# Two small tiles are padded, and all large tiles begin at other addresses

## The chip, the cores and the metric

The kernel runs on one core of a Trainium2 chip. The metric is device time in microseconds of one execution, taken as the median of several runs; lower is better. TensorE (PE) multiplies, VectorE (DVE) and ScalarE (ACT) work elementwise, and SyncE (SP) issues the transfers from memory (HBM) to the on-chip memory. A tile has 128 partitions (rows) and a number of bytes in each; "address" below means the byte offset of a tile within each partition, and "residue" that offset modulo 512.

## What is computed

A trunk of two decoder layers over 512 tokens of width 1024, all in float32. Layer 0 mixes tokens with a Mamba-2 block (SSD), layer 1 with HGRN2; each layer has a squared-ReLU MLP and a gate by an embedding of its own:

```python
for i in range(DEPTH):                       # DEPTH = 2
    mix = ssd_mixer(x, ...) if i % 2 == 0 else hgrn2_mixer(x, ...)
    h = layer_norm(DEEPNORM_ALPHA * x + mix, ln_g[i, 0], ln_b[i, 0])
    h = layer_norm(DEEPNORM_ALPHA * h + sq_relu_mlp(h, mlp_w1[i], mlp_w2[i]), ln_g[i, 1], ln_b[i, 1])
    x = h + jax.nn.sigmoid(h @ ple_w_gate[i]) * (p[i] @ ple_w_proj[i])

def sq_relu_mlp(h, w1, w2):
    a = jax.nn.relu(h @ w1)                  # 1024 -> 4096
    return (a * a) @ w2
```

SSD projects to 5152 columns, convolves, computes decayed scores in chunks of 128 tokens for 32 heads, norms and projects back. HGRN2 projects to 4096 columns and works on 8 heads with a decay for each key channel, then norms and gates.

## The kernel before

Almost all time goes into products of weights and activations. For precision each operand is split into a high and a low part of type float32r, and a product is made of three matmuls that accumulate in one bank of PSUM (helper `mm3`, lines 110 to 112: high by high, high by low, low by high). In a matmul one operand is stationary (loaded into the array, 128 columns at a time) and the other moves through it, 512 or 256 columns at a time.

- `unit` (line 98) brings a weight unit of 128 x 1024 values: a transfer into a slot `raw`, a copy by ScalarE into `whi` (line 104), the rest by VectorE into `wlo` (line 106). There are 3 slots of raw and 5 each of whi and wlo.
- Activations lie transposed and split in slots of `b8` (9 slots of 8192 bytes, class `Split`).
- `project` takes the weights as stationary and b8 as moving operand; `out_part` takes b8 as stationary and whi or wlo as moving operand.
- In the MLP of each layer most pairs of hidden tiles are made with Strassen's scheme (`strassen`, 7 products of 256 columns for 8). Four of its seven left factors are sums of blocks: three of them lie in the tiles `S`, the fourth in a slot of b8; the other three are read from b8 as they are.
- The HGRN phase has its order on TensorE written out by hand: the projections of later heads fill the waits of a head's scores (`fill`, `need`, `background`). Its 128-column products (line 782: scores; lines 869, 880, 882: states and outputs) are plain float32, and the profile shows two records for each. In the SSD phase lines 522, 561, 591 and 596 are of the same kind; transposes (lines 200, 516, 549 and others) go through TensorE with `ident` from the constants as moving operand.

Tiles come from pools. The pools `consts`, `raws`, `whip`, `wlop`, `b8`, `accp`, `w4` and `sm` are placed one behind another in the order in which they are opened, and last the pool of the temporaries of the running phase (`tmp`: xs, sz, cv, cm, cbm, z, S, y, pv and so on), which is exchanged at each phase. Each tile's place is rounded up to 32 bytes. Two of the small tiles are `one`, a column of ones in `consts` (used as a bias when `ones_r` is filled), and `hri`, four reciprocals per head of HGRN in `sm`, which has two slots for each of its names.

Of the kernel before, what the change touches and what calls it, by code (L numbers as in the profile page):

```python
# [15 lines left out]
P = 128  # L16
T = 512
NCH = 4
# [11 lines left out]
# the first pairs of hidden tiles are plain products, the others Strassen's  # L30
PLAIN = 3
ORDER = [(w[0], int(w[1])) for w in "h0 b0 h1 o0 h2 o1 h3 o2 h4 o3 h5 o4 h6 o5 h7 o6 o7".split()]
# HGRN: the projections in their order, and how much of them goes between the steps of two heads
# [9 lines left out]
def trunk(ctx: ExitStack, tc, a):  # L43
# [9 lines left out]
    sm = pool("sm", 2)  # L53
# [21 lines left out]
    def begin(name):  # L75
        """the pool of temporaries of a phase, in place of the phase before's"""
        if phase:
            phase[1].__exit__(None, None, None)
            phase.clear()
        phase.append(tc.tile_pool(name=name, bufs=1, reuse_waits="tile"))  # L80
        phase.append(phase[0].__enter__())
        phase.reverse()
        phase.append(bufs[name])
# [13 lines left out]
    # ---------------------------------------------------------------- weights  # L97
# [16 lines left out]
    class Split:  # L114
        """[128, n, 512] as high and low parts, in slots of four rows each."""
# [11 lines left out]
    def project(src, xs, ps, m=P, tok=slice(0, T)):  # L127
        """ps[m, tok] = W[:, tile].T @ x.T for a weight unit of eight row tiles."""
        hi, lo = src
        for k in range(8):  # L130
            c = slice(k * m, (k + 1) * m)
            mm3(ps[:m, tok], hi[:, c], lo[:, c], xs.h(k, tok), xs.l(k, tok), k == 0, k == 7)

    # ---------------------------------------------------------------- constants
# [30 lines left out]
    one = mk(cpool, [P, 1], "one")  # L165
# [4 lines left out]
    # ---------------------------------------------------------------- layer norm and friends  # L170
# [7 lines left out]
    def layer_norm(c, gb):  # L178
        """acc[:, c] = LN(acc[:, c])"""
        src = acc[:, c, :]  # L180
        st = mk(sm, [P, 2, 6], "lnst")
        for h in range(2):
            nc.vector.bn_stats(st[:, h, :], src[:, h * 512 : (h + 1) * 512])
        mv = mk(sm, [P, 2], "lnmv")
        nc.vector.bn_aggr(mv, st.rearrange("p a b -> p (a b)"))
        sd = mk(sm, [P, 1], "lnsd")
        nc.scalar.activation(sd, mv[:, 1:2], AF.Sqrt, bias=eps)
        rs = mk(sm, [P, 1], "lnrs")
        nc.vector.reciprocal(rs, sd)
        nc.vector.scalar_tensor_tensor(src, src, mv[:, 0:1], gb[0], ALU.subtract, ALU.mult)  # L190
        nc.vector.scalar_tensor_tensor(src, src, rs, gb[1], ALU.mult, ALU.add)

    def transpose_split(src, dst, c, keep=None):
        """dst[:, k, chunk c] = src[tokens, k-th 128 features].T, split; unsplit in keep"""
        sl = slice(c * P, (c + 1) * P)
        for q in range(2):
            pt = bank(pst, "pt")
            for j in range(4):
                k = 4 * q + j
                nc.tensor.transpose(pt[:, j * P : (j + 1) * P], src[:, k * P : (k + 1) * P], ident)  # L200
            v = pt.rearrange("p (j t) -> p j t", j=4)
            h = dst.hi[q][:, :, sl]
            nc.scalar.copy(h, v)
            nc.vector.tensor_sub(dst.lo[q][:, :, sl], v, f32(h))
            if keep is not None:
                nc.scalar.copy(keep[q][:, :, sl], v)

    def out_part(units, n, xs, c, h, first, scale):
        """acc[:, c, half h] += x[:, chunk c].T @ W over n row tiles, each token's row by scale if given;
        acc holds alpha * residual (or the residual, if first)"""  # L210
        sl = slice(c * P, (c + 1) * P)
        ps = bank(psj, "pj")
        for k in range(n):
            hi, lo = units[k // 2]
            ks = slice((k % 2) * 512, (k % 2 + 1) * 512)
            mm3(ps, xs.h(k, sl), xs.l(k, sl), hi[:, ks], lo[:, ks], k == 0, k == n - 1)
        d = acc[:, c, h * 512 : (h + 1) * 512]
        if scale is not None:
            nc.vector.scalar_tensor_tensor(d, ps, scale[:, c : c + 1], d, ALU.mult, ALU.add)
        elif first:  # L220
            nc.vector.scalar_tensor_tensor(d, d, ALPHA, ps, ALU.mult, ALU.add)
        else:
            nc.vector.tensor_add(d, ps, d)  # L223

    def out_project(w, xs, first, after=None, scale=None):
        """w: the four units of four row tiles, by halves of the columns; after(c): what follows the last of chunk c"""
        if after is not None:
            units = [unit(w[i]) for i in range(4)]
            for c in range(NCH):
                for h in range(2):  # L230
                    out_part(units[2 * h : 2 * h + 2], 4, xs, c, h, first, scale)
                after(c)
        else:
            for h in range(2):
                units = [unit(w[2 * h + i]) for i in range(2)]
                for c in range(NCH):
                    out_part(units, 4, xs, c, h, first, scale)

    def norm(i):
        """the norm's result, transposed and split, and what makes its chunk c"""  # L240
        gb = ln_params(i)
        h_s = Split(8)
        keep = [mk(b8, [P, 4, T], "b8") for _ in range(2)] if i % 2 == 0 else None

        def chunk(c):
            layer_norm(c, gb)
            transpose_split(acc[:, c, :], h_s, c, keep)

        return h_s, chunk, keep

    # Winograd's form of Strassen's product: seven products of blocks for eight. The blocks of h.T are
    # [token half][k half], those of the weights [k half][output tile].
    def block_sums(h_s, ht):
        """the four plain and four summed blocks of h.T, as (high, low) of a row tile k"""
# [28 lines left out]
    def weight_sums(src1, src2):  # L283
        """the seven blocks of two weight units: B11, B21, B22, T1, T2, T3, B21 - T2, as (high, low, column)"""
# [24 lines left out]
    def strassen(blocks, src1, src2, z):  # L309
        """z[:, m] = W[:, tile m].T @ h.T for two weight units"""  # L310
# [34 lines left out]
    def mlp_and_gate(layer, h_s, ht, last):  # L345
        """acc holds the normed h. Returns the next x, transposed and split, with x in acc."""
# [40 lines left out]
        # gate  # L387
# [45 lines left out]
    # ---------------------------------------------------------------- layer 0: SSD  # L433
    # time steps
# [36 lines left out]
    # dt * exp(cs_last - cs)  # L471
# [6 lines left out]
    def dt_tail():  # L478
        # token-major copies: [128 tokens, chunk, head]
# [10 lines left out]
    def conv_silu(ps, i, out):  # L490
        """out = silu(causal conv of ps + bias), channel tile i of the convolved ones"""
        cv = tmp("cv", [P, T])
        nc.scalar.activation(cv, ps, AF.Identity, scale=convw[:, i, 3:4], bias=convb[:, i : i + 1])
        for k in range(3):
            d = 3 - k
            nc.vector.scalar_tensor_tensor(cv[:, d:], ps[:, : T - d], convw[:, i, k : k + 1], cv[:, d:], ALU.mult, ALU.add)
        nc.scalar.activation(out, cv, AF.Silu)
# [44 lines left out]
    def core(j, xs, sz, y, toks, btok, cbm, cm):  # L542
# [3 lines left out]
        # token-major x * dt and x * dt * decay to the chunk's end  # L546
# [11 lines left out]
        # chunk states and their scan  # L558
# [13 lines left out]
        # masked decays times C B  # L572
# [9 lines left out]
        # decay from the chunk's start, on channels  # L582
# [33 lines left out]
    def rms_group(ss):  # L616
        """1 / rms of each token of the group: [128 tokens, chunk]"""
# [52 lines left out]
    # ---------------------------------------------------------------- layer 1: HGRN2  # L670
# [6 lines left out]
    # lower bounds: softmax over the one layer, cumulated, less its first row  # L677
# [11 lines left out]
    # The tensor engine's order is fixed here: the projections of the heads to come fill the waits of a head's scores.  # L689
    def vg(i):  # L690
        """values and output gates of heads 2i and 2i + 1, by tokens: [128, chunk, 256]"""
# [80 lines left out]
    def hcore(h, s, i, hl):  # L772
# [12 lines left out]
        def column_sums(f, n):  # L785
            """the sums over the partitions, on each of them"""
# [8 lines left out]
        # the scores of a token with itself and of an odd one with the token before it  # L795
# [63 lines left out]
        # states  # L859
# [23 lines left out]
        # norm and output gate  # L883
# [5 lines left out]
        ri = mk(sm, [P, NCH], "hri")  # L889
# [51 lines left out]
def _tiles_m(w):  # L941
    """[K, M] -> [M/128, 128, K/128 * 128]: one unit per 128 output channels"""
# [4 lines left out]
def _tiles_g(w):  # L947
    """[K, 1024] -> [K/128, 128, 1024]: per four row tiles, two units for each half of the columns"""
# [5 lines left out]
def _tiles_h(w):  # L954
    """[K, 1024] -> [2 * K/256, 128, 2 * 512]: by halves of the columns, two row tiles each"""
# [5 lines left out]
def _tiles_q(w):  # L961
    """[1024, 1024] -> [4, 2, 128, 4 * 256]: by quarters of the columns, four row tiles each"""
# [4 lines left out]
def _cols(v):  # L967
    """[n * 128] -> [128, n]"""
# [3 lines left out]
def _rows(v):  # L972
    """[K, T] -> [128, K/128, T]"""
# [70 lines left out]
```

## Time and profile before

| | us |
|---|---|
| median of 3 runs | 1495.58 |
| lowest and highest run | 1493.39, 1496.82 |
| the profiled execution: span from its first to its last instruction | 1492.3 |
| TensorE busy in it | 1479.3 (99%) |
| VectorE busy | 1096.4 (73%) |
| ScalarE busy | 711.2 (48%) |

The page gives no other time for the profiled execution than its span; the runs lie 1.1 to 4.5 us above it. The granted TensorE clock is full (0.999 on average). Groups of the profile are read as: line, engine, operation, tile written <- tiles read (the moving operand of a matmul first), shape, count | busy time in us, mean ns of one | idle time before them. A matmul's own duration is a latency, and matmuls overlap; how fast they follow each other is read from their starts in the timeline. The name `b` in a row stands for a slot of b8 or for the second tile of w4.

The SSD phase takes roughly the first 350 us, the MLP and gate of layer 0 go up to about 790, HGRN up to about 1090, and the MLP and gate of layer 1 fill the rest.

### The profile page before, as it was taken

To read this page: it belongs to the slowest core of one execution; us is meant where nothing else is said; L and a number is where in the kernel's file an instruction comes from. 1 tells how busy PE (TensorE), PEld (TensorE's weight loads), DVE (VectorE), ACT (ScalarE), POOL (GpSimd) and SP (SyncE) were. 2 spreads that over 40 slices of the span, in tenths; PEclk is the share of its full clock that TensorE was granted. 3 is DMA by queue.
4 is the path that set the end of the run, shared out by engine and by line. 5 is a ranking of instruction groups with operands and counts; after the bars stand their busy time and mean duration, and the time that the engine had idled before them with its cause. 6 is when DMAs were issued, how large, how long until landed. Compare 5 with 4: busy or idle time off the path is not lost.

```text
span 1492.3 us, 21964 instructions
## 1 busy us (share of the span) xinstructions
PE 1479.3 (99%) x8848; PEld 1280.9 (86%) x8848; DVE 1096.4 (73%) x1786; ACT 711.2 (48%) x968; POOL 0.9 (0%) x8
## 2 busy tenths in 40 slices
PE   8999999999999999999999999999999999999998
PEld 5888888888989999888778998989898999998887
DVE  6998677797886777776844767769787777777673
ACT  5777455563564434444334453543364444444342
POOL 0000000000000000000000000000000000000000
PEclk9999999999999999999999999999999999999999
DMA  6433223332233323244223222222123333324322
GB/s 237 169 102 111 98 100 113 100 113 85 71 99 99 113 82 103 88 139 129 94 71 114 86 66 77 70 72 72 57 72 99 114 113 100 110 79 150 115 71 71
DMA packets 41621, 150.07 MB, mean 101 GB/s; under 512 B 4624, under 2 KB 5136, under 8 KB 41392
## 3 DMA queue, kind: packets, MB, share of 16 engines
q1 hardware_dynamic: 41520, 148.67, 30.1%
q8 instruction: 70, 1.15, 0.3%
q14 instruction: 31, 0.25, 0.1%
HBM read 146.49 MB, written 2.16 MB: 100 GB/s over the span
## 4 chain that ended last, share of the span: by engine, by line
PE 97%; DMA 1%; DVE 1%; ACT 1%; issue 0%; SPq 0%; ACTq 0%; DVEq 0%
PE pj L110 29%; PE pj L111 28%; PE pj L112 28%; PE py L782 1%; PE py L591 1%; PE pt L200 1%; PE pm L561 1%; PE py L596 1%; PE py L792 1%; PE py L827 1%; DMA raw<-in_wg 1%; DVE wlo L106 0%; PE pt L549 0%; PE py L880 0%; PE py L112 0%; PE py L110 0%
## 5 line engine op out<-in xcount | busy, mean ns | idle before, releaser
L110 PE MATMUL pj<-whi,b 128*128 128x512 f32 (+1 forms) x1096 | 401.5, 367 | 0.5 <-ACT z L414 0.5
L111 PE MATMUL pj<-wlo,b 128*128 128x512 f32 (+1 forms) x1096 | 399.3, 364 | 0.5 <-DVE wlo L106 0.5
L112 PE MATMUL pj<-whi,b 128*128 128x512 f32 (+1 forms) x1096 | 399.8, 365 | 0.0
L110 PE MATMUL pj<-b,whi 128*128 128x256 f32 (+1 forms) x1024 | 348.0, 340 | 2.1 <-ACT whi L104 2.1
L112 PE MATMUL pj<-b,wlo 128*128 128x256 f32 (+1 forms) x1024 | 344.2, 336 | 0.0
L111 PE MATMUL pj<-b,whi 128*128 128x256 f32 (+1 forms) x1024 | 343.7, 336 | 0.0
L104 ACT CAST whi<-raw 128x1024 fp32r<-128x1024 f32 x192 | 201.4, 1050 | 229.6 <-PE pj L111 133.4
L106 DVE TENSOR_TENSOR wlo<-raw,whi 128x1024 fp32r<-128x1024 f32 x192 | 233.9, 1220 | 64.4 <-ACT whi L104 62.4
L111 PEld LDWEIGHTS pj<-wlo,b 128*128 128x128 f32 x1096 | 206.8, 189 | 32.2 <-DVE wlo L106 1.0
L110 PEld LDWEIGHTS pj<-whi,b 128*128 128x128 f32 x1096 | 206.6, 189 | 32.3 <-ACT z L414 0.7
L112 PEld LDWEIGHTS pj<-whi,b 128*128 128x128 f32 x1096 | 206.7, 189 | 31.7 <-issue 0.2
L110 PEld LDWEIGHTS pj<-b,whi 128*128 128x128 f32 x1024 | 194.5, 190 | 22.0 <-ACT whi L104 4.7
L112 PEld LDWEIGHTS pj<-b,wlo 128*128 128x128 f32 x1024 | 194.4, 190 | 20.3 <-DVE b L150 1.7
L111 PEld LDWEIGHTS pj<-b,whi 128*128 128x128 f32 x1024 | 194.6, 190 | 18.3 <-issue 1.9
L293 ACT CAST whi<-raw 128x1024 fp32r<-128x1024 f32 (+1 forms) x52 | 43.4, 835 | 136.2 <-PE pj L112 110.4
L223 DVE TENSOR_TENSOR acc<-pj,acc 128x512 f32<-128x512 f32 x120 | 81.6, 686 | 35.0 <-PE pj L112 34.5
L110 PE MATMUL pj<-S,whi 128*128 128x256 f32 x312 | 87.4, 280 | 0.0
L111 PE MATMUL pj<-S,whi 128*128 128x256 f32 x312 | 87.0, 279 | 0.0
L112 PE MATMUL pj<-S,wlo 128*128 128x256 f32 x312 | 87.0, 279 | 0.0
L295 DVE TENSOR_TENSOR wlo<-raw,whi 128x1024 fp32r<-128x1024 f32 (+1 forms) x52 | 49.7, 957 | 35.0 <-ACT whi L293 35.0
L293 ACT CAST whi<-a 128x1024 fp32r<-128x1024 f32 x26 | 27.3, 1050 | 94.8 <-PE pj L111 45.5
L110 PEld LDWEIGHTS pj<-S,whi 128*128 128x128 f32 x312 | 58.7, 188 | 0.0
(217 smaller groups left out, 1810.6 us busy)
## 6 DMA issues: line engine op xcount, KB each, us to landing
raw<-in_w SPq DMA_DIRECT2D x128, 512.0 KB, 3.4
raw<-in_wssd SPq DMA_DIRECT2D x40, 512.0 KB, 3.4
a<-csd SPq DMA_DIRECT2D x16, 512.0 KB, 4.0
raw<-in_wso SPq DMA_DIRECT2D x16, 512.0 KB, 3.3
raw<-in_wg SPq DMA_DIRECT2D x16, 512.0 KB, 3.8
raw<-in_whvg SPq DMA_DIRECT2D x16, 512.0 KB, 3.3
raw<-in_whq SPq DMA_DIRECT2D x16, 512.0 KB, 3.3
raw<-in_who SPq DMA_DIRECT2D x8, 512.0 KB, 3.3
```

Source lines behind the costliest of these rows:

```text
L104: nc.scalar.copy(hi[:, :n], raw[:, :n])
L106: nc.vector.tensor_sub(lo[:, :n], raw[:, :n], f32(hi[:, :n]))
L110: nc.tensor.matmul(out, sh, mh, start=start, stop=False)
L111: nc.tensor.matmul(out, sh, ml, start=False, stop=False)
L112: nc.tensor.matmul(out, sl, mh, start=False, stop=stop)
L200: nc.tensor.transpose(pt[:, j * P : (j + 1) * P], src[:, k * P : (k + 1) * P], ident)
L223: nc.vector.tensor_add(d, ps, d)
L293: nc.scalar.copy(hi[:, :n], f)
L295: nc.vector.tensor_sub(lo[:, :n], f, f32(hi[:, :n]))
L561: nc.tensor.matmul(pst_[:, c * P : (c + 1) * P], btok[:, c, :], xw[:, c].rearrange("p h q -> p (h q)"), start=True, stop=True)
L591: nc.tensor.matmul(yd[64 * r : 64 * r + 64, sl], xdt[:, 2 * c + r, :], m[:, r, sl], start=True, stop=True)
L596: nc.tensor.matmul(yo[:, c * P : (c + 1) * P], pv[:, c - 1].rearrange("p h q -> p (h q)"), cm[:, c * P : (c + 1) * P], start=True, stop=True,)
```

## The change

Two tiles are allocated larger than what is used of them; the used part is a view of the first columns. All other lines differ only in comments, which are left out.

```diff
-    one = mk(cpool, [P, 1], "one")
+    one = mk(cpool, [P, 16], "one")[:, 0:1]
     nc.gpsimd.memset(one, 1.0)
...
         nc.scalar.activation(ms, ms, AF.Sqrt, scale=1.0 / P, bias=eps)
-        ri = mk(sm, [P, NCH], "hri")
+        ri = mk(sm, [P, 64], "hri")[:, :NCH]
         nc.vector.reciprocal(ri, ms)
```

Four bytes of `one` become 64 in each partition, and 16 bytes of `hri` become 256, in each of its two slots. With the rounding to 32 bytes, the tiles behind `one` move by 32 bytes, and those behind `hri` by 448 more. The slots from `raws` to `w4` go from residue 480 to 0, those of the phase pools from 32 to 0.

## The prediction

> **What bounds the kernel now.** I read the page first (busy shares, then the chain that ended last), then the groups kept apart by shape, then single rows of the timeline, and last the windows.
>
> ```profile
> span 1492.3 us, 21964 instructions
> PE 1479.3 (99%) x8848; PEld 1280.9 (86%) x8848; DVE 1096.4 (73%) x1786; ACT 711.2 (48%) x968; POOL 0.9 (0%) x8
> PE 97%; DMA 1%; DVE 1%; ACT 1%; issue 0%; SPq 0%; ACTq 0%; DVEq 0%
> ```
>
> TensorE is busy for 99% of the span, and the chain of waits runs through it for 97%. So the time is the number of matmuls times the step from the start of one to the start of the next, plus some 45 us (3% of 1492.3) in which TensorE waits. A change that adds no work and removes none can only act through that step, or through those 45 us. The counts by shape:
>
> ```profile
> L110 PE MATMUL pj<-whi,b 128*128 128x512 f32 x824 | 323.4, 393 | 0.0
> L110 PE MATMUL pj<-b,whi 128*128 128x512 f32 x480 | 194.2, 405 | 2.1 <-ACT whi L104 2.1
> L110 PE MATMUL py<-whi,a 128*128 128x512 f32 x32 | 12.7, 398 | 0.0
> L110 PE MATMUL pj<-b,whi 128*128 128x256 f32 x544 | 153.7, 283 | 0.0
> L110 PE MATMUL pj<-whi,b 128*128 128x256 f32 x272 | 78.1, 287 | 0.5 <-ACT z L414 0.5
> L110 PE MATMUL pj<-S,whi 128*128 128x256 f32 x312 | 87.4, 280 | 0.0
> L591 PE MATMUL py<-b,xdt 128*64 128x128 f32 x256 | 22.0, 284 | 0.0
> L880 PE MATMUL py<-a,cm 128*128 128x128 f32 x64 | 11.0, 274 | 0.0
> L869 PE MATMUL pm<-a,btok 128*128 128x128 f32 x48 | 6.8, 278 | 0.5 <-DVE pv L873 0.5
> ```
>
> Helper mm3 issues each product three times (L110, L111, L112), so these rows stand for 3 x (824 + 480 + 32) = 4008 products of 512 columns, 3 x (544 + 272) = 2448 of 256 columns whose moving operand (the first name after the arrow) lies in a slot of b8, whi or wlo, and 3 x 312 = 936 of 256 columns whose moving operand is S. The mean ns of a row are latencies of overlapping matmuls; the step has to be read from the starts in the timeline:
>
> ```profile
> 802.95 0.39 PE L112 MATMUL pj<-b,wlo 128*128 128x512 f32 x1
> ...
> 809.75 0.39 PE L112 MATMUL pj<-b,wlo 128*128 128x512 f32 x1
> ```
>
> ```profile
> 408.95 0.28 PE L110 MATMUL pj<-b,whi 128*128 128x256 f32 x1
> ...
> 412.79 0.28 PE L112 MATMUL pj<-b,wlo 128*128 128x256 f32 x1
> ```
>
> ```profile
> 425.25 0.28 PE L110 MATMUL pj<-S,whi 128*128 128x256 f32 x1
> ...
> 429.38 0.28 PE L112 MATMUL pj<-S,wlo 128*128 128x256 f32 x1
> ```
>
> Between the two rows lie 30, 32 and 35 steps: 6.80/30 = 226.7 ns for 512 columns, 3.84/32 = 120.0 ns for 256 columns out of b8, 4.13/35 = 118.0 ns for 256 columns out of S. The first two give the price of a column, (226.7 - 120.0)/256 = 0.417 ns, hence 213.3 and 106.7 ns of pure streaming. What is left is the same for both widths: 13.3 ns a matmul, as long as 32 columns (128 bytes of a row). With S it is 118.0 - 106.7 = 11.3 ns. Over the kernel this fixed part is 4008 x 13.3 + 2448 x 13.3 + 936 x 11.3 = 53.3 + 32.6 + 10.6 = 96 us, the only large amount that a mere shift of addresses could touch.
>
> **The change, part by part.** The program places its tiles in the order of declaration, each rounded up to 32 bytes. From their sizes, the constants begin 128 bytes past a multiple of 512 (16,512 bytes in), and all slots from raws to w4 (raw, whi, wlo, b8, acc, a, b) at 480 past one; their sizes are multiples of 4096, so all share that residue. The tiles of the phases (S, xs, z and so on) begin at 32 past a multiple. Tile one grows from 32 to 64 bytes: everything behind it moves by 32, and the big slots land at residue 0. The two slots of hri grow from 32 to 256 bytes each: the phase tiles move by 32 + 448 = 480, and land at 0 too. No instruction is added, removed or moved: the memset of one still writes one column, and ri is still four columns wide. No wait is added, and nothing goes past SP's or POOL's queue. These edits cost nothing by themselves.
>
> What may change is what each access costs. The important fact is that the trace has products that differ in the residue of the moving operand: b8 at 480 costs 120.0 ns, S at 32 costs 118.0, with the same shape, the same weights tiles, the same three lines. So the start matters by nanoseconds. I take the simplest reading: the fixed part is mostly one surplus fetch because a row does not begin where a fetch begins, and it goes when it does. No product in the trace has a moving operand of the large kind on residue 0, so the saving has to be bounded:
>
> Upper bound, 512 columns: all 13.3 ns, to 213.3. For 256 columns another limit comes first. Each matmul has its own weight load, and the 128-column products, which stream for only 53 ns, show at what step loads follow each other:
>
> ```profile
> 849.54 1.05 PE L782 MATMUL py<-xs,cv 128*128 128x128 f32 x8
> 49.09 0.49 PE L516 MATMUL pt<-cst,bm 128*128 128x128 f32 x3
> ```
>
> Eight records in 1.05 us with some 0.275 for the last (0.274 and 0.278 in the rows above) make (1.05 - 0.275)/7 = 111 ns; the transposes of L516 make (0.49 - 0.275)/2 = 108 ns. I let the 256-column products stop at 111: 9.0 ns saved out of b8, 7.0 out of S. The upper sum is 4008 x 13.3 + 2448 x 9.0 + 936 x 7.0 = 53.3 + 22.0 + 6.6 = 82 us. Lower bound of the same reading: only what 480 against 32 shows, 2 ns on 6456 products = 13 us. From below nothing: if the start is not the reason, 0, and a loss is priced under the rivals. I take the upper sum as the pace, because a constant of exactly 32 columns that is the same at both widths looks like a unit of fetching and not like a remainder.
>
> The Trainium skill (TensorE: Matmul & The Clock Gate, "Wait — 56ns, not 53.3ns?") puts a back-to-back matmul at its columns over 2.4 GHz plus about 2.5 ns, measured in bf16. The trace agrees on the columns (0.417 ns each) and not on the rest (13.3 ns); if 2.5 ns stay, the 512-column term is 4008 x 10.8 = 43 us by that page instead of 53.3, and the sum 72 instead of 82.
>
> Not all of this arrives at the end, since TensorE then asks for weights and evictions sooner:
>
> ```profile
> 30.00:400.00 370.00, 369.97 (x2029) 303.03 (x2028) 301.96 (x564) 216.50 (x285) 0.00 (x0) 1.00 0.32 107
> 400.00:700.00 300.00, 300.00 (x1891) 272.70 (x1891) 220.66 (x306) 140.58 (x156) 0.00 (x0) 1.00 0.33 106
> 800.00:1090.00 290.00, 289.28 (x1972) 255.72 (x1971) 207.72 (x418) 130.69 (x260) 0.00 (x0) 1.00 0.22 72
> 1090.00:1400.00 310.00, 310.00 (x1977) 282.67 (x1976) 229.59 (x319) 144.73 (x162) 0.00 (x0) 1.00 0.33 108
> ```
>
> In these windows (columns: length, then busy PE, PEld, DVE, ACT, POOL, then clock, DMA share, GB/s) VectorE is busy for 302 of 370, 221 of 300, 208 of 290 and 230 of 310 us. A stage shorter by 6% leaves it at 87% in the first and at 78% at most in the others, so it does not become the bound; the clock is 1.00 throughout, and the DMA share about a third. But in the first and third window products wait in chains through VectorE and ScalarE, which do not get shorter, and the places where only a transfer counts (here the three longest) stay as they are:
>
> ```profile
> 729.14 4.47 DMA raw<-in_wg
> 760.41 3.58 DMA raw<-in_wg
> 790.45 3.83 DMA raw<-in_whq
> ```
>
> These rows are from the chain in order of time. The first and third window hold 370 + 290 = 660 of 1492 us, so some 44% of the 82 us, 36, are saved there; I let two fifths of that, 15 us, be given back to the chains (my choice; the ends are nothing and all of the 36). Net 67 us. Against the profile's span that is 1492.3 - 67 = 1425; the median of the runs, 1495.6, lies 3.3 us above the span, so **1428 us**.
>
> **The rivals.** First, the forecast in part (chance 0.23): the fixed part belongs to changing the weights, and only the 2 ns that tell S from b8, up to 5 ns, hang on the start. 2 to 5 ns on 6456 products are 13 to 32 us: 1464 to 1483 us, middle 1475. For it: S improves by only 2 ns although its start differs by 64 bytes. Against it: 13.3 is so exactly 32 columns.
>
> Second, no effect (0.14): the 13.3 ns are a switch between products, and S is quicker for another reason, such as its two parts lying in one tile; 1495.6. For it: in all these rows the residue of b8, whi and wlo is one and the same, so none shows a change of it. Against it: the transposes of L516, whose moving operand is a constant that begins 128 past a multiple of 512, step at 108 ns, the products of L782, whose moving operand begins 32 past one, at 111. The Trainium skill (SBUF — State Buffer, "Specifications (TRN2)") speaks for this rival: its lines are 16 bytes, and 480 and 32 are multiples of 16, so by that rule nothing begins askew now. The 2 ns between S and b8 are what the page does not explain. That the tiles do not land where I worked it out (0.03) gives the same time.
>
> Third, slower (0.16): what counts is not the start but the distance between the starts of the two streams, weights and moving operand, because both are fetched at once. Now S and whi lie 64 bytes apart and cost 118.0, b8 and whi at equal residues cost 120.0. After the change all residues are equal: the 936 S products pay 2 ns more, 1.9 us, and so may the 256 + 64 + 48 = 368 records of L591, L880 and L869, which mix an a or b slot (480) with a phase tile (32) and now get equal residues, at up to 4 ns (111 against 108): 1.5 us. That is 1495.6 + 3.4 = 1499. It decides where the extra exceeds 2.3 ns on these 1304 matmuls. Against it: the distances among the big slots stay what they are, so 6456 of the products keep theirs.
>
> **How the numbers follow.** A measurement of this kernel can tell about 0.2%, 3 us, from no change. Forecast 0.44, in part 0.23: faster 0.67. No effect 0.14 and not placed so 0.03: same 0.17. Slower 0.16. The forecast's own range reaches from 1404 to 1445: at the low end nothing is given back and the loads follow each other at 108 ns, which adds 3 x 3384 = 10 us (1495.6 - 92); at the high end 3 ns of the fixed part stay at 512 columns (12 us less) and 20 us are given back (1495.6 - 50). The range that should hold 8 in 10 goes from 1404 through the partial case to the top of no effect, 1497; it leaves out the slower case and a little below.
>
> **What would show it.** In the profile after: steps of 512-column products at 213 to 217 ns and of 256-column ones at 108 to 113, S equal to b8; PE still at 98 to 99% of a shorter span; the same counts of instructions; DVE's busy time about 1096 us and its share up by three points; the waits of raw<-in_wg no shorter. A step of 224 and 118 would be the partial case, 226.7 and 120.0 with S at 118.0 no effect, and S at 120.0 with the rest unchanged the slower rival. If PE's share falls under 96%, the give-back is mis-sized. The prediction is wrong as a whole if the step of the 512-column products does not move.

## The result and the profile after

The changed kernel takes 1497.32 us (median of 15 runs, 1494.92 to 1498.94) against 1494.67 us of the kernel before on the same chip (15 runs, 1492.72 to 1496.82): 1.0015 times the time, 95% interval 1.0008 to 1.0022. It is slower by 2.65 us, where 67 us less had been forecast. The profiled execution of it begins like this (span, busy shares, chain that ended last by engine):

```profile
span 1494.8 us, 21964 instructions
PE 1481.7 (99%) x8848; PEld 1283.0 (86%) x8848; DVE 1096.8 (73%) x1786; ACT 710.9 (48%) x968; POOL 0.9 (0%) x8
PE 97%; DMA 1%; DVE 1%; ACT 1%; issue 0%; SPq 0%; ACTq 0%; DVEq 0%
```

The counts are those of before, and the instructions of each engine stand in the same order. The span grew by 2.5 us (from 1492.3), TensorE's busy time by 2.4 us (from 1479.3): the loss is TensorE's. Apart by shape, in the view of the groups:

```profile
L110 PE MATMUL pj<-whi,b 128*128 128x512 f32 x824 | 323.3, 393 | 0.2 <-ACT whi L104 0.2
L110 PE MATMUL pj<-b,whi 128*128 128x512 f32 x480 | 194.4, 405 | 1.7 <-ACT whi L104 1.7
L110 PE MATMUL pj<-b,whi 128*128 128x256 f32 x544 | 153.7, 283 | 0.0
L110 PE MATMUL pj<-S,whi 128*128 128x256 f32 x312 | 88.3, 283 | 0.0
L591 PE MATMUL py<-b,xdt 128*64 128x128 f32 x256 | 22.0, 284 | 0.0
```

Of these only the row of S moves: 88.3 us instead of 87.4, and on mm3's two other lines 88.3 instead of 87.0. The other rows shown stand within 0.2 us. The timeline gives the step, first for 512 columns, then for 256 columns out of b8, then out of S:

```profile
803.69 0.39 PE L112 MATMUL pj<-b,wlo 128*128 128x512 f32 x1
...
809.81 0.39 PE L112 MATMUL pj<-b,wlo 128*128 128x512 f32 x1
```

```profile
408.73 0.28 PE L110 MATMUL pj<-b,whi 128*128 128x256 f32 x1
...
412.57 0.28 PE L112 MATMUL pj<-b,wlo 128*128 128x256 f32 x1
```

```profile
425.02 0.28 PE L110 MATMUL pj<-S,whi 128*128 128x256 f32 x1
...
429.11 0.28 PE L111 MATMUL pj<-S,whi 128*128 128x256 f32 x1
```

Between the rows lie 27, 32 and 34 steps: 6.12/27 = 226.7 ns, 3.84/32 = 120.0 ns, and 4.09/34 = 120.3 ns, where before stood 118.0. Over the whole trace 932 of the 936 S products step at exactly 120 ns. So what came is the third rival's picture: S became as slow as b8, and no other step changed by more than 0.2 ns in the mean. 936 x 2.1 ns = 2.0 us of the 2.5 us. The three longest waits for a transfer grew too, in the chain in order of time:

```profile
729.83 4.82 DMA raw<-in_wg
761.43 3.76 DMA raw<-in_wg
791.65 4.05 DMA raw<-in_whq
```

They were 4.47, 3.58 and 3.83 us, together 0.75 less. But they are not the rest: TensorE's idle time, span less busy time, grew only from 13.0 to 13.1 us. Where the other half microsecond lies, and whether it hangs on the change, no run shows.

### The profile page after: what moved, and what is told of

Read it like the earlier page. It is cut to its first block, busy times and chain, and to the rows that moved or that the text cites. A ratio compares the mean times of both kernels' runs of the same rounds, so it can differ in the third digit from the quotient of the medians.

```text
span 1494.8 us, 21964 instructions
## 1 busy us (share of the span) xinstructions
PE 1481.7 (99%) x8848; PEld 1283.0 (86%) x8848; DVE 1096.8 (73%) x1786; ACT 710.9 (48%) x968; POOL 0.9 (0%) x8
## 4 chain that ended last, share of the span: by engine, by line
PE 97%; DMA 1%; DVE 1%; ACT 1%; issue 0%; SPq 0%; ACTq 0%; DVEq 0%
PE pj L110 29%; PE pj L111 28%; PE pj L112 28%; PE py L782 1%; PE py L591 1%; PE pt L200 1%; PE pm L561 1%; PE py L596 1%; PE py L792 1%; PE py L827 1%; DMA raw<-in_wg 1%; DVE wlo L106 0%; PE pt L549 0%; PE py L880 0%; PE py L112 0%; PE py L111 0%
## 5 line engine op out<-in xcount | busy, mean ns | idle before, releaser
L112 PE MATMUL pj<-S,wlo 128*128 128x256 f32 x312 | 88.3, 283 | 0.0
L110 PE MATMUL pj<-S,whi 128*128 128x256 f32 x312 | 88.3, 283 | 0.0
L111 PE MATMUL pj<-S,whi 128*128 128x256 f32 x312 | 88.3, 283 | 0.0
L112 PEld LDWEIGHTS pj<-S,wlo 128*128 128x128 f32 x312 | 59.9, 192 | 0.0
```

Source lines behind the costliest of these rows:

```text
L110: nc.tensor.matmul(out, sh, mh, start=start, stop=False)
L111: nc.tensor.matmul(out, sh, ml, start=False, stop=False)
L112: nc.tensor.matmul(out, sl, mh, start=False, stop=stop)
```

## The experiments

Each edit is against the kernel before, unless it says otherwise. "Distance" is the start of the moving operand less the start of the weights (or whatever is stationary), in bytes of a partition, modulo 512. Steps called means are taken from all starts of a shape in a trace, leaving out gaps (over 150 ns for 256 columns, over 260 for 512). The traces hold no addresses: which slot a product reads is worked out from the order in which the kernel asks for tiles.

**The start, or the distance.** In the changed kernel S has both a new start (0 for 32) and a new distance from whi (0 for 64). Padding `one` to 512 bytes gives S the new start and leaves it the old distance.

```diff
-    one = mk(cpool, [P, 1], "one")
+    one = mk(cpool, [P, 128], "one")[:, 0:1]
```

> Only tile one is widened, to 512 bytes: the big slots (raw to w4) go to residue 448 and the phase tiles to 0, so S and whi stay 64 bytes apart as in before, but S itself begins at 0 as in after. Theory 'distance' (the step depends on how far the starts of the moving operand and of the weights lie apart): S products step at 118.0 ns as before, all others as before, median as before (1494.7, within 2 us). Theory 'start' (a moving operand that begins at residue 0 costs 120 whatever the weights do): S products step at 120.0 ns as in after, median 1497.

Measured: 1495.08 us against 1495.99, ratio 0.9992 (0.9983 to 1.0002). The timeline, 33 steps of S:

```profile
426.31 0.28 PE L111 MATMUL pj<-S,whi 128*128 128x256 f32 x1
...
430.20 0.28 PE L111 MATMUL pj<-S,whi 128*128 128x256 f32 x1
```

3.89/33 = 117.9 ns. With S at residue 0 and 64 bytes from the weights it is as quick as before. S begins at the very same address here and in the changed kernel (480 bytes past where it began before), so its own start can't explain 117.9 against 120.0 ns. The start at a multiple of 512 does nothing; the distance does.

**One half of the change, then the other.** With `one` alone padded, the big slots land at 0 and S at 64; with `hri` alone, both land at 480.

```diff
-    one = mk(cpool, [P, 1], "one")
+    one = mk(cpool, [P, 16], "one")[:, 0:1]
```

> Only tile one is padded (32 bytes more): big slots at 0, phase tiles at 64. Theory 'distance': the distance of S and whi is 64 as in before, S steps at 118.0 ns, median as before (1494.7, within 2 us). Theory 'start', that residue 32 was lucky for S: S steps at 120.0 ns unless residue 64 is lucky too, median about 1497.

Measured: 1495.48 us against 1495.99, 0.9998 (0.9988 to 1.0007); S steps at 118 ns.

```diff
-        ri = mk(sm, [P, NCH], "hri")
+        ri = mk(sm, [P, 64], "hri")[:, :NCH]
```

> Only hri is padded: big slots stay at residue 480 as in before, and the phase tiles move to 480 too. Theory 'distance': S and whi at distance 0, S steps at 120.0 as in the changed kernel, median as there (1497, 0.15% over before): this half of the change makes the whole loss. Theory 'start' (residue 0 costs): S begins at 480 where b8 began in before, 120.0 too; the two theories differ in e1, not here. If the loss needs both halves: 1495 as before.

Measured: 1497.97 us against 1495.69, 1.0012 (1.0003 to 1.0021); all 936 S products step at exactly 120.0 ns. The padding of `hri` makes the loss by itself, although the slots and the phase tiles then begin at residue 480 and none of them at 0.

**Is there a start at which the surplus vanishes?** Two kernels spread the starts of the b8 slots: one in steps of 64 bytes (slots 64 bytes longer), one in steps of 4 (slots 128 bytes longer, the used part 0 to 124 bytes in). Both have the whole change besides.

```diff
-            self.hi = [mk(b8, [P, 4, T], "b8", F32R) for _ in range((n + 3) // 4)]
+            self.hi = [slot8r(F32R) for _ in range((n + 3) // 4)]    # all b8 slots alike
...
+        t = mk(b8, [P, 2048 + 16], "b8", dt)         # steps of 64 bytes
+        return t[:, 0:2048]
...
+        t = mk(b8, [P, 2048 + 32], "b8", dt)         # steps of 4 bytes
+        o = (5 * nb8[0]) % 32
+        return t[:, o : o + 2048]
```

> The changed kernel, with the slots of b8 64 bytes longer, so that the nine slots begin at residues 0, 64, 128 to 448 and 0 again, while whi and wlo stay at 0. One profile then holds products of 512 and of 256 columns at each distance of 64 bytes. Theory 'distance': the step differs by slot; at distance 0 120.0 and 226.7 ns, at +64 bytes of the moving operand 118.0 and 224.7; whether further distances save more is open, and at best the whole fixed part goes (106.7 and 213.3). Theory 'switch' (13.3 ns are the price of changing the weights, and S is quicker because its two parts share a tile): all b8 slots step at 120.0 and 226.7 whatever their residue.

Measured: 1502.79 us (one run; before 1495.99). The step now differs from slot to slot: the mean of 512-column products goes up (228.4 to 230.3 ns with b8 moving, 227.5 to 231.0 with whi), that of 256-column products with b8 moving down (120.0 to 118.0). Short stretches of up to 9 products ran at 113.3 ns; the kernels with a gap, below, show that step at distance 192.

> The changed kernel, with b8 slots of 8320 bytes whose used part begins at 0 to 124 bytes past their start in steps of 4, so that moving operands and weights out of b8 begin at all multiples of 4 bytes modulo 512; whi and wlo stay at 0. Theory 'surplus fetch at the start' (what the prediction assumed, on a unit finer than 512 bytes): the step of b8 products changes with the start modulo 16, 32 or 64, by several ns. Theory 'distance': it changes with the distance in pieces of 64 bytes only, and starts off a multiple of 16 cost nothing of their own.

Measured: 1509.12 us (one run). Mean steps by the moving start modulo 16:

| start mod 16 | 512 columns, ns | 256 columns, ns |
|---|---|---|
| 0 | 231.2 | 118.6 |
| 4 | 235.3 | 119.9 |
| 8 | 230.4 | 119.6 |
| 12 | 231.4 | 119.1 |

With b8 stationary the 512-column step is 231.5 to 232.3 at all four. No start brings it near 213: the fixed part isn't a fetch that a better start would save. (Start and distance move together here, since whi and wlo lie at 0, so the 235.3 ns belong to either.) The Trainium skill (SBUF — State Buffer, "Operand start alignment") asks only that an operand start at a multiple of its element size, and says that its runs timed nothing; here starts 4 bytes apart are timed, and none is a quick one by itself.

**The distance by itself.** Four kernels keep everything at one uniform distance: `one` goes into a pool of its own between the weights' slots and b8, and grows by 64 bytes at a time. Only the distances between weights, b8 and S change; the order of the instructions does not.

```diff
-    b8 = pool("b8", 9)
+    gap = pool("gap", 1); b8 = pool("b8", 9)
...
-    one = mk(cpool, [P, 1], "one")
+    one = mk(gap, [P, 16], "one")[:, 0:1]       # 16, 32, 48, 64: 64 to 256 bytes
```

> The kernel before, with tile one in a pool of its own between wlo and b8, 64 bytes long: b8 begins 64 bytes past whi and wlo (modulo 512), the phase tiles 128 past them; the same instructions in the same order. Theory 'distance': 256-column products out of b8 step like S in before, 118.0 ns; S at distance 128 takes another value, not known; 512-column products of project (b8 moving, +64) at 224.7 to 226.7, those of out_part (whi moving, -64 = 448) unknown, up to 233 by the mixed rows of e3. Theory 'switch': 120.0 and 226.7 everywhere, S at 118.

> The same with 128 bytes: b8 at +128, S at +192. Theory 'distance': S steps at 113.3 ns, the value that e3 reached in stretches where all distances were 192; b8 at 256 columns between 113 and 120. 936 S products at 4.7 ns less are 4.4 us. Theory 'switch': 120.0, 226.7, and S at 118.

> The same with 192 bytes: b8 at +192, S at +256. Theory 'distance': 256-column products out of b8 step at 113.3 ns, 1632 x 6.7 = 11 us less than before; S unknown; the 512-column products of project at 226.7 - 6.7 = 220.0 if the gain does not depend on the width, those of out_part (whi moving, -192 = 320) unknown. If e3's mixed rows tell the sign, out_part steps at up to 233 and eats the gain: 2472 x 6 = 15 us. Theory 'switch': as before.

> The same with 256 bytes: b8 and whi half a period of 512 apart, so that project and out_part have the same distance of 256 whichever moves; S at +320. Theory 'distance': one value for all 512-column products, unlike 226.7, and another for 256 columns, unlike 120.0; if half a period is the best case, the whole sum falls by up to 6.7 ns x 6456 = 43 us. Theory 'switch': as before, 1495.

Measured, against 1495.50 us of before: 1503.63 us with 64 bytes (1.0053, 1.0033 to 1.0073), 1504.66 with 128 (1.0052, 1.0029 to 1.0075), 1497.90 with 192 (1.0012, 1.0000 to 1.0023), 1495.02 with 256 (0.9995, 0.9983 to 1.0006). Mean steps by distance, from these four and the kernels before and after:

| distance | 256 columns, ns | 512 columns, ns |
|---|---|---|
| 0 | 119.9 to 120.0 (b8, S), 119.4 to 119.6 (whi) | 227.5 (whi moving), 228.4 (b8) |
| 64 | 117.8 to 117.9 | 229.5 (b8) |
| 128 | 118.6 to 119.0 | 232.2 (b8) |
| 192 | 114.0 to 114.3 | 233.3 (b8) |
| 256 | 119.5 to 119.9 | 227.4 (whi), 228.3 (b8) |
| 320 | 117.8 to 117.9 | 229.1 (whi) |
| 384 | 118.8 | 232.4 (whi) |
| 448 | 114.0 (whi) | 233.3 (whi) |

The lower half of the table repeats the upper one: only the distance modulo 256 counts. The two widths want opposite things: of these distances 192 is the best for 256 columns and the worst for 512. Two things expected did not come: 192 cost the 512-column products of `project` 5 ns instead of saving 6.7, and half of 512 gave the values of distance 0. Single rows of the timeline show it: S at distance 192 (kernel with 128 bytes), then b8 with 512 columns at 192 and at 256 (kernels with 192 and 256 bytes), then whi moving against b8 at 448 (kernel with 64 bytes).

```profile
462.76 0.28 PE L112 MATMUL pj<-S,wlo 128*128 128x256 f32 x1
...
466.04 0.28 PE L111 MATMUL pj<-S,whi 128*128 128x256 f32 x1
```

```profile
805.80 0.39 PE L111 MATMUL pj<-b,whi 128*128 128x512 f32 x1
...
811.87 0.39 PE L110 MATMUL pj<-b,whi 128*128 128x512 f32 x1
```

```profile
805.77 0.39 PE L110 MATMUL pj<-b,whi 128*128 128x512 f32 x1
...
811.89 0.39 PE L110 MATMUL pj<-b,whi 128*128 128x512 f32 x1
```

```profile
354.71 0.40 PE L110 MATMUL pj<-whi,b 128*128 128x512 f32 x1
...
358.91 0.40 PE L110 MATMUL pj<-whi,b 128*128 128x512 f32 x1
```

They lie 29, 26, 27 and 18 steps apart: 113.1, 233.5, 226.7 and 233.3 ns. The groups of the kernel with 192 bytes show both signs in one program, where before stood 153.7 and 194.2 us:

```profile
L110 PE MATMUL pj<-b,whi 128*128 128x256 f32 x544 | 150.6, 277 | 0.0
L110 PE MATMUL pj<-b,whi 128*128 128x512 f32 x480 | 196.5, 409 | 1.9 <-ACT whi L104 1.9
```

The steps come near the times. With 64 bytes, in products times the change of the step: 1440 x 1.1 (b8, 512 columns, 64) + 2472 x 5.8 (whi, 512, 448) + 936 x 0.8 (S, 128) - 1632 x 2.1 (b8, 256, 64) - 816 x 5.4 (whi, 256, 448) = 1.6 + 14.3 + 0.7 - 3.4 - 4.4 = 8.8 us; measured 8.1. The same working gives 12.1 us with 128 bytes and 1.5 with 192, where 9.2 and 2.4 were measured.

The Trainium skill (SBUF — State Buffer, "Who interferes with whom") gives TensorE two independent read ports, one for the moving operand and one for loading weights, and says that it never waits on anyone. By that no distance should matter; here the step differs by 6 to 7 ns between distances 0 and 192, so for these float32r products the two streams aren't independent in time. What they share was not seen, only that where one begins against the other counts. Nor do these kernels tell whether a product's own weights count or those loaded for the next one meanwhile, since both lie at one distance.

**Finer distances.** The changed kernel, with whi and wlo slots 256 bytes longer and each run of products at one offset of 0 to 240 bytes in steps of 16:

```diff
+    def off():
+        nu[0] += 1
+        return 4 * (nu[0] % 16)
...
-            hi = mk(whip, [P, 1024], "whi", F32R)
+            hi = mk(whip, [P, 1088], "whi", F32R)[:, o : o + 1024]    # lo alike
```

> The changed kernel with slots of whi and wlo of 4352 bytes (a multiple of 256), whose used part begins at an offset of 0, 16, 32 to 240 bytes, the same for all units that one run of products reads and another for the next. So every run of 12 to 96 products has one distance, and one profile holds the step at 16 distances for both widths. Theory 'distance with a period of 256 bytes' (from e5 to e8): multiples of 64 give again 120, 118, 119, 113 to 114 ns at 256 columns (distance 0, 64, 128, 192) and 227, 229, 232, 233 at 512; what lies between is open: a straight course between them if the overlap of two streams counts by bytes, steps if it counts by 64-byte pieces. Theory 'switch': no course at all.

Measured: 1509.26 us (one run; before 1495.69). Mean steps in ns by distance modulo 256 (a dash where too few products had it):

```text
distance      0    16    32    48    64    80    96   112   128   144   160   176   192   208   224   240
256 col.  120.0 117.8 116.6 116.7     - 118.1 119.8 117.8     - 119.9 118.6 119.5 114.3 119.0 118.3 118.3
512 col.  227.7 231.4 233.1 232.5 230.0 230.8 233.6 232.1 232.8 233.3 234.0 232.5 233.3 233.9 233.1 234.8
```

Neither a straight course nor one in steps of 64 bytes: 0 stands alone as the best of 512 columns, with 64 next, and 192 as the best of 256. The first column of each row shows again that a distance of 0 is the mapping that the 4008 long products want, and that they had it before the change.

**A version for both widths.** The changed kernel, with each product given the distance that its width wants: 0 for 512 columns, 192 for most of the 256-column products (weights 64 bytes in, so that the moving operand begins 64 bytes before them, or 192 bytes in where the weights move).

```diff
-    def unit(src, lead=LEAD):
+    def unit(src, lead=LEAD, o=0):
...
-            hi = mk(whip, [P, 1024], "whi", F32R)
+            hi = mk(whip, [P, 1088], "whi", F32R)[:, o : o + 1024]    # lo alike
...
-    def weight_sums(src1, src2):
+    def weight_sums(src1, src2, o=16):
...
-                    us.append((unit(w1[j]), bank(psj, "pj")))
+                    us.append((unit(w1[j], o=16), bank(psj, "pj")))
...
-            units = [unit(a["whvg"][4 * i + 2 * which + j]) for j in range(2)]
+            units = [unit(a["whvg"][4 * i + 2 * which + j], o=48) for j in range(2)]
```

> The changed kernel with slots of whi and wlo of 4352 bytes, used from byte 64 on for the weights of Strassen's products and of the first four units of each MLP, and from byte 192 on for the units of vg, so that all products of 256 columns have the distance 192 (modulo 256) and those of 512 columns keep distance 0. Theory 'distance': 256-column steps at 113.5 ns, so against before 1248 x 6.4 + 936 x 4.4 + 384 x 6 + 768 x 5.5 = 8.0 + 4.1 + 2.3 + 4.2 = 18.6 us less: about 1477, and 512 columns at 226.7 as before. Theory 'switch': 1497 as the changed kernel.

Measured: 1488.67 us against 1495.69, 0.9950 (0.9937 to 0.9964): half a per cent faster than the kernel before, and below the changed kernel's 1497.32. The page of the profile:

```profile
PE 1472.7 (99%) x8848; PEld 1274.3 (86%) x8848; DVE 1095.9 (74%) x1786; ACT 710.8 (48%) x968; POOL 0.9 (0%) x8
```

TensorE is 9.0 us less busy than after the change, and the span is 8.8 us shorter (1486.0): what the step saves arrives, nothing is given back. The 512-column steps stay at 227.4 and 228.5 ns. But 7.0 us is less than half of the 18.6 expected: the 256-column steps came to 117.8 ns (S), 117.3 (b8) and 115.9 (weights moving), and not to 113 to 114.

**Why not 113.** Here the slots are 4352 bytes long, so that neighbours differ by 256 modulo 512, which the gap kernels' slots did not. Slots of 4608 bytes, a multiple of 512, take that difference away (three small tiles move to the pool of temporaries to make room; the edit is against the version for both widths):

```diff
-            hi = mk(whip, [P, 1088], "whi", F32R)[:, o : o + 1024]
+            hi = mk(whip, [P, 1152], "whi", F32R)[:, o : o + 1024]    # lo alike
...
-            t = mk(cpool, [P, NCH, 32], tag)
+            t = tmp(tag, [P, NCH, 32])
```

> As e10, but the slots of whi and wlo are 4608 bytes (a multiple of 512), so that the distance modulo 512 is the same for the high and the low weights; the three small tiles dt_tok, w_tok and cs_tok move into the pool of the SSD phase to make the room. In e10 a product's distance changed between 192 and 448 from one product to the next, and the step was 117.8 and not the 113 to 114 that both distances gave alone in e5, e6 and e7. Theory 'distance modulo 512, and the same from product to product': Strassen's products at 113.3 to 114.3 ns, 512 columns at 226.7 to 227.5, so against before 1248 x 6 + 936 x 4 + 384 x 6 + 768 x 5.5 = 17.7 us less: 1478, and 10 less than e10. If the low value comes from something else in e5 to e7: 117.8 and 1488.7 as e10.

Measured: 1490.27 us against 1495.64, 0.9961 (0.9947 to 0.9975). That was not it. The timeline shows two steps at one and the same distance, each of them lasting:

```profile
390.73 0.28 PE L112 MATMUL pj<-b,wlo 128*128 128x256 f32 x1
...
392.77 0.28 PE L112 MATMUL pj<-b,wlo 128*128 128x256 f32 x1
```

```profile
426.16 0.28 PE L110 MATMUL pj<-S,whi 128*128 128x256 f32 x1
...
430.17 0.28 PE L111 MATMUL pj<-S,whi 128*128 128x256 f32 x1
```

2.04/18 = 113.3 ns in the MLP's first pairs, 4.01/34 = 117.9 ns in Strassen's products. The quick stretch runs through 54 products, the slow ones through up to 167.

The last experiment asked whether a run of products takes its step from how it is entered: the weights B11 and B21 of each Strassen pair go back to distance 0, so that the products at 192 follow products at 0. The edit is against the kernel just above, where `split` now takes the offset as an argument.

```diff
-            w1 = split(r1)
+            w1 = split(r1, o=0)
```

> As e12, but the first of the four weight tiles of a Strassen call (blocks B11 and B21) is used from byte 0, so that the first and the fifth of its seven products run at distance 0 and the others at 192: each call enters distance 192 twice out of 256-column products at distance 0. In e12 the same distance showed two lasting steps, 113.3 to 114 and 117.8 ns, and kept one of them for up to 167 products; in e6 and e7, where distances changed within a call, it was mostly the quick one. Theory 'the step is chosen on entering': the products at distance 192 step at 113.5 and the 24 at distance 0 at 120, per call 24 x 120 + 60 x 113.5 = 9.69 us against 84 x 117.8 = 9.90, 26 calls: 5.3 us less than e12, about 1485. Theory 'the step goes with the absolute places of the tiles': 117.8 and 120, 1.4 us more than e12, about 1491.5.

Measured: 1491.16 us against 1495.86, 0.9968 (0.9956 to 0.9980). The products at 0 step at 119.8 ns, those at 192 stay at 117.8, so entry from distance 0 does not choose the quick step. The time is near the one that the theory of fixed places gave, but the trace of the kernel before this one (slots of 4608 bytes) speaks against that theory. In the products of `vg` the step changes where two sums of line 792 come between:

```profile
835.90 0.28 PE L112 MATMUL pj<-whi,b 128*128 128x256 f32 x1
...
837.60 0.28 PE L112 MATMUL pj<-whi,b 128*128 128x256 f32 x1
837.72 0.39 PE L792 MATMUL py<-b,ones_r 128*128 128x256 f32 x2
837.95 0.28 PE L110 MATMUL pj<-whi,b 128*128 128x256 f32 x1
...
838.89 0.28 PE L112 MATMUL pj<-whi,b 128*128 128x256 f32 x1
```

15 steps before the sums make 1.70/15 = 113.3 ns, 8 steps behind them 0.94/8 = 117.5. By the order of the tiles, the slow products read the same weights from the same addresses as quick ones at 834.5 to 836.2 us had done, and the same two slots of b8, 512 bytes further on. So what comes right ahead matters, and in a pattern. Of the stretches of at least eight products, in this trace and in that of the version for both widths alike, all 18 that follow a 512-column product of mm3 directly stay slow, all 8 behind a pair of 512-column sums turn quick within five products, and 4 of 5 behind a pair of 256-column sums stay slow. No run varied this by itself, so why one entry gives one step and another the other stays open.

## Why the prediction was wrong

**What bounds the kernel** was right: TensorE at 99%, and a change that adds no instruction acts through the step. Only the 45 us in which TensorE was to wait were too many: span less busy time was 1492.3 - 1479.3 = 13.0 us. The placement was right too: all big slots and phase tiles landed at residue 0 as worked out, and nothing on SP's or POOL's queue moved.

**The step that failed** is "I take the simplest reading: the fixed part is mostly one surplus fetch because a row does not begin where a fetch begins". Three runs speak against it: S at residue 0 keeps its 117.9 ns when the distance is 64; the 512-column products at residue 0 keep their 226.7; and starts 4 bytes apart have no quick one among them. The 82 us of the upper sum were therefore nothing at all. In the place of the start the runs put the distance between the moving operand and the weights: it went from 64 to 0 for S, which took its step from 117.9 to 120.0 ns, and stayed as it was for the other 6456 products. The evidence for the failed reading was one number (13.3 ns is as long as 32 columns) and one pair of rows (S against b8). That pair differed in two things, the start and the distance from the weights, and the prediction gave the price to the start and named the distance only under the rivals. That the rest was "the same at both widths" was no evidence at all: a price per column and a rest can always be fitted to two widths. At distance 192 the same working gives (233.3 - 113.3)/256 = 0.469 ns a column and a rest of -6.7 ns.

**L516 against L782**, 108 against 111 ns, was held up against the rival of no effect. These products have other weights and other distances as well, so the comparison told nothing of the start.

**The third rival** had the mechanism and nearly the price. Its first term, 936 x 2 ns = 1.9 us, was measured at 2.0. Its second, up to 1.5 us on the 368 records of L591, L880 and L869, did not come: their groups stand at 22.0, 11.1 and 6.8 us against 22.0, 11.0 and 6.8. It gave 3.4 us, 2.65 were measured; that the totals lie so near is in part luck, since 1.5 of the one never came and some 0.6 of the other has no known place. Its counter-argument, that the distances among the big slots stay, was right and is why the loss is small. It was no reason against the sign.

**The other rivals.** The partial case fell with the start. No effect would have been right for all but S.

**What was given back** could not be tested at the size of 82 us. At 9.0 us, in the version for both widths, the span shortened by 8.8. Of these some 768 x 3.7 ns = 2.8 us lie in the products of `vg`, in the third window, and hardly any in the first. So the two fifths were too much for the third window at this size, and the first was not put to the test.

**What stays beside the columns.** By the Trainium skill (TensorE: Matmul & The Clock Gate, "Wait — 56ns, not 53.3ns?") 2.5 ns would remain beside the columns; with 0.417 ns a column the traces leave 13.3 at distance 0, and from 6.6 to 20.0 at the other multiples of 64. The Trainium skill (SBUF — State Buffer, "Specifications (TRN2)") spoke for no effect with its lines of 16 bytes. For starts at multiples of 16 that agrees with the runs (S at 117.9 ns from residues 32, 0 and 64); of the distance, by which S lost its 2 ns, that section says nothing.

## What to carry to other kernels

Before a constant rest of a step is put down to an address, find two groups of rows that differ in that address alone, or make them: here two rows differed in the start and in the distance to the other operand, and one padded tile would have parted the two. Where float32r matmuls follow each other without gaps, the start of the moving operand against that of the stationary one, modulo 256 bytes, is a setting worth mapping by shape, since here the best value for one width was among the worst for another; rounding everything to one boundary picks the value 0 for all. A shift of addresses that adds no instruction is still a change of the bound when 7,392 products take their step from it.

## What the runs showed of the hardware that was not expected

- The step of float32r products depends on the distance of the two operands' starts, with a period of 256 bytes: 120.0 ns at 0 and 113.3 at the best for 256 columns, 226.7 at 0 and 233.3 at 192 for 512 columns. From 0 to 192 the one step falls by 6.7 ns and the other rises by 6.6, each about the time of 16 columns at the 0.417 ns that distance 0 gives.
- At distance 192 the 256-column products have two lasting steps, 113.3 and 117.8 ns, in one program. In the kernels with a gap 82 to 88% were at 113 to 114 (means 114.0 to 114.3); with weights' offsets that differ between products most were at 117.8. Neither the slots' difference of 256 bytes nor entry from distance 0 selects between them. One trace has both steps on the same weights and slots, and all 18 stretches directly behind 512-column products of mm3 were slow, so what comes right ahead has a part in it; how stays open.
- Absolute starts showed no effect of their own where the distance was kept: S stepped at 117.9 ns from residues 32, 0 and 64. Of starts in steps of 4 bytes none was quick.
